# Splitting one tile's load by partitions, with short late copies, in a DMA-bound prefix log-sum-exp kernel

## The chip, the cores and the metric

The kernel runs on one core of one Trainium2 chip. The metric is the device time of one execution in microseconds (us), on the slowest core (here the only one).

## The reference

The input `x` is float32 of shape (4, 4096, 4128). For each of the 4 batches and each of the 4128 columns, the output is the running log-sum-exp down the 4096 rows:

```
out[:, 0, :] = x[:, 0, :]
for t in range(1, S):
    mx = max(out[:, t-1, :], x[:, t, :])
    out[:, t, :] = mx + log(exp(out[:, t-1, :] - mx) + exp(x[:, t, :] - mx))
```

It reads 270.5 MB and writes 270.5 MB, each byte once.

## The kernel before

Each of 44 steps loads one tile: 128 partitions, in each of them `r` consecutive rows of one batch (r is 3 in 40 steps, 2 in 4 steps; the first step has 2). ScalarE (ACT) takes exp, TensorE multiplies by triangular matrices of ones to form the running sums in PSUM (here the tiles `pt` and `qt`, which the matmuls write), and ACT takes the log back into the tile, which is stored. VectorE keeps the last row as a carry for the next step. SP issues all loads and stores on one hardware queue. There are four tile buffers.

```python
    class Step:
        def dram(self, t):
            rows = t[self.b, self.row:self.row + P * self.r, :]
            return rows.rearrange("(p j) d -> p j d", j=self.r)   # partition p: r whole rows

        def load(self):
            full = xpool.tile([P, R, D], FP32, name="xt")
            self.xt = full[:, :self.r, :]
            self.half = self.xt.bitcast(FP16)
            nc.sync.dma_start(out=self.xt, in_=self.dram(x))

        def store(self):
            nc.sync.dma_start(out=self.dram(out), in_=self.xt)
    # ... cut: Chunk, which does exp, the matmuls, the log and the carry ...
    ahead = bufs - 1                       # 3
    for s in steps[:ahead]:
        s.load()
    for n, s in enumerate(steps):
        # ... cut: the compute of the step ...
        s.store()
        if n + ahead < len(steps):
            steps[n + ahead].load()
```

One partition of a three-row tile is one contiguous run of 3 x 4128 x 4 = 49,536 bytes in HBM, and the trace shows it as one DMA packet. A whole tile is 128 packets (10,240 for the 80 three-row transfers), 8 for each of the 16 DMA engines.

The softmax here doesn't subtract the row's maximum and nothing guards it: scores larger than these inputs give would overflow.

## Time and profile before

| | before |
|---|---|
| time, median of 3 (later runs: 1263.1 to 1263.4) | 1263.23 us |
| profiled span | 1261.7 us |
| busy: DMA engines / ACT / TensorE / VectorE | 99% / 77% / 54% / 36% |
| a 49,536-byte packet, median | 1.829 us |
| first exp starts | 13.0 us |
| last store issued | 1243.7 us |

From the page of the kernel before: the mean busy share of the 16 DMA engines in 40 equal slices of the span (tenths), what they moved, and the hardware queue (packets, MB, share of 16 engines' span).

```profile
DMA  9999999999999999999999999999999999999997
GB/s 410 410 443 432 425 432 439 432 428 432 436 433 431 433 436 431 431 438 431 436 434 431 429 432 438 434 429 432 431 440 431 433 430 430 437 433 431 434 429 328
q1 hardware_dynamic: 12672, 541.07, 99.4%
```

The DMA engines are busy in every slice; compute is not what holds the run. The next fence is busy time by stretch: the stretch, its length, then busy us and instruction count of each engine, the granted clock, the busy share of the DMA engines, and GB/s in the last column.

```profile
core 0: us, PE busy (x) PEld busy (x) DVE busy (x) ACT busy (x) POOL busy (x), PEclk, DMA share, GB/s
0.00:34.00 34.00, 11.14 (x27) 3.71 (x28) 11.96 (x15) 19.22 (x15) 2.17 (x13) 1.00 0.95 404
34.00:54.00 20.00, 15.10 (x44) 5.30 (x44) 5.13 (x5) 16.36 (x12) 0.00 (x0) 0.91 1.01 412
54.00:84.00 30.00, 17.83 (x65) 6.48 (x64) 10.54 (x12) 24.46 (x20) 0.00 (x0) 0.77 1.03 446
84.00:1262.00 1178.00, 642.81 (x2135) 230.02 (x2134) 423.81 (x415) 916.58 (x688) 0.00 (x0) 0.75 0.99 430
```

From the page's list of DMA issues of before: KB of one, median us from issue to landing.

```profile
xt<-in_x_dram SPq DMA_DIRECT2D x40, 6192.0 KB, 43.7
xt<-in_x_dram SPq DMA_DIRECT2D x4, 4128.0 KB, 39.1
```

A load lands some 44 us after its issue, three transfers of 14.6 us, so two others are ahead of it in the queue. The chain of waits of before (start, duration, what) shows the first load landing at 13.0 us:

```profile
0.80 12.20 DMA xt<-in_x_dram
```

The queue's issue times on SP (start, duration, line, what), early and late:

```profile
0.80 1.33 SPq L112 DMA_DIRECT2D xt<-in_x_dram  x3
31.72 0.35 SPq L115 DMA_DIRECT2D out_dram<-xt  x1
32.11 0.45 SPq L112 DMA_DIRECT2D xt<-in_x_dram  x1
...
1223.92 20.17 SPq L115 DMA_DIRECT2D out_dram<-xt  x2
```

The last line covers the last two stores, issued at 1223.9 and 1243.7 us.

### The profile page before, as it was taken

The numbers are of one execution on the slowest core, as the hardware profiler recorded it, in microseconds if no ns is written. First come the engines' busy times: TensorE is split into PE (matmuls) and PEld (weight loads), VectorE is DVE, ScalarE is ACT, GpSimd is POOL, SyncE is SP. The second block draws the span as 40 slices with busy tenths as digits, with TensorE's granted clock in tenths as the row PEclk, the third lists the DMA queues.
The fourth block names the chain that finished last, engine by engine and source line by source line (L and its number), as shares of the span: only waits on it lengthen the run. The fifth ranks groups of instructions, "written<-read, shape, count | busy, mean of one in ns | idle before, by whom it ended". The sixth has DMA issues, their size and how long they took to land.

```text
span 1261.7 us, 6165 instructions
## 1 busy us (share of the span) xinstructions
PE 686.9 (54%) x2268; PEld 245.5 (19%) x2268; DVE 451.4 (36%) x445; ACT 976.6 (77%) x733; POOL 2.2 (0%) x13
## 2 busy tenths in 40 slices
PE   3566566566555554545456565554545656545452
PEld 1122222122121221111112222111211212111120
DVE  3433343433333433343333343334333334343333
ACT  5888887888787878778678887877867887787783
POOL 0000000000000000000000000000000000000000
PEclk9977777777677778787667777878766777787876
DMA  9999999999999999999999999999999999999997
GB/s 410 410 443 432 425 432 439 432 428 432 436 433 431 433 436 431 431 438 431 436 434 431 429 432 438 434 429 432 431 440 431 433 430 430 437 433 431 434 429 328
DMA packets 12702, 541.46 MB, mean 429 GB/s; under 512 B 1408, under 2 KB 1408, under 8 KB 1408
## 3 DMA queue, kind: packets, MB, share of 16 engines
q1 hardware_dynamic: 12672, 541.07, 99.4%
q8 instruction: 18, 0.29, 0.1%
q14 instruction: 12, 0.10, 0.0%
HBM read 270.53 MB, written 270.53 MB: 429 GB/s over the span
## 4 chain that ended last, share of the span: by engine, by line
DMA 50%; ACT 25%; PE 20%; issue 2%; DVE 1%; ACTq 0%; SPq 0%
DMA xt<-in_x_dram 29%; DMA out_dram<-xt 21%; PE pt L87 20%; ACT xt L161 13%; ACT xt L127 11%; ACT xt L166 0%; DVE carry L91 0%; DVE carry L92 0%; PE qt L87 0%; ACTq L227 0%; SPq L112 0%; ACTq L127 0%
## 5 line engine op out<-in xcount | busy, mean ns | idle before, releaser
L161 ACT ACTIVATE xt<-pt 128x1024 f32<-128x1024 f32 x512 | 504.7, 1025 | 159.1 <-PE pt L87 87.0
L127 ACT ACTIVATE xt<-xt 128x3072 f16<-128x3072 f32 (+3 forms) x176 | 475.3, 2701 | 76.9 <-DMA xt<-in_x_dram 75.4
L91 DVE CAST carry<-pt 32x1024 f16<-32x1024 f32 x176 | 216.4, 1230 | 695.2 <-ACT xt L161 690.6
L87 PE MATMUL pt<-xt,ident 128*128 128x512 f16 x672 | 235.4, 437 | 313.1 <-ACT xt L161 312.6
L87 PE MATMUL pt<-xt,incl 128*128 128x512 f16 x352 | 157.3, 543 | 242.6 <-ACT xt L127 241.9
L87 PE MATMUL pt<-xt,excl 128*128 128x512 f16 x672 | 263.1, 531 | 0.0
L92 DVE TENSOR_TENSOR carry<-pt,carry 32x1024 f16<-32x1024 f32 x176 | 215.9, 1227 | 6.1
L87 PEld LDWEIGHTS <-ident 128*128 128x128 f16 x672 | 67.0, 103 | 451.1 <-issue 423.0
L87 PEld LDWEIGHTS <-excl 128*128 128x128 f16 x756 | 95.3, 128 | 149.8 <-issue 122.9
L87 PE MATMUL pt<-carry,pick 128*128 128x512 f16 x320 | 119.7, 463 | 0.0
L87 PEld LDWEIGHTS <-incl 128*128 128x128 f16 x480 | 51.8, 112 | 330.6 <-issue 281.2
L87 PEld LDWEIGHTS <-pick 128*128 128x128 f16 x360 | 42.7, 119 | 65.0 <-issue 48.3
L91 DVE CAST carry_t<-qt 32x32 f16<-32x32 f32 x44 | 8.7, 197 | 90.8 <-ACT xt L166 90.7
L166 ACT ACTIVATE xt<-qt 128x96 f32<-128x96 f32 (+1 forms) x44 | 10.9, 249 | 30.3 <-PE pt L87 30.3
L87 PE MATMUL qt<-xt,incl 128*128 128x64 f16 (+2 forms) x128 | 12.2, 195 | 0.0
L87 PE MATMUL qt<-xt,excl 128*128 128x64 f16 (+1 forms) x84 | 10.6, 186 | 0.0
L92 DVE TENSOR_TENSOR carry_t<-qt,carry_t 32x32 f16<-32x32 f32 x44 | 8.5, 194 | 1.5
L87 PE MATMUL qt<-carry_t,pick 128*128 128x96 f16 (+1 forms) x40 | 8.1, 202 | 0.0
L82 DVE MEMSET carry<- 128x512 uint32 x4 | 1.9, 485 | 1.1 <-PEq L216 1.0
L69 ACT ACT_TABLE_LOAD x1 | 1.3, 1283 | 0.8 <-PEq L216 0.8
L35 POOL TENSOR_SCALAR_AFFINE_SELECT pick<-pick 128x128 f16<-128x128 f16 x2 | 0.6, 296 | 0.1
L35 POOL TENSOR_SCALAR_AFFINE_SELECT ident<-ident 128x128 f16<-128x128 f16 x1 | 0.3, 298 | 0.0
(11 smaller groups left out, 1.9 us busy)
## 6 DMA issues: line engine op xcount, KB each, us to landing
xt<-in_x_dram SPq DMA_DIRECT2D x40, 6192.0 KB, 43.7
out_dram<-xt SPq DMA_DIRECT2D x40, 6192.0 KB, 43.5
xt<-in_x_dram SPq DMA_DIRECT2D x4, 4128.0 KB, 39.1
out_dram<-xt SPq DMA_DIRECT2D x4, 4128.0 KB, 34.0
```

The source lines that it names most:

```text
L35: nc.gpsimd.affine_select(out=t, in_=t, pattern=[[step, P]], compare_op=mybir.AluOpType.not_equal, fill=1.0, base=base, channel_multiplier=1,)
L69: nc.scalar.preload_act_table_set("natural_log_exp_and_others")
L82: nc.vector.memset(t, 0.0)
L87: nc.tensor.matmul(pt, lhsT=w, rhs=rhs, start=start, stop=stop, skip_group_check=True)
L91: nc.vector.tensor_copy(cr[HI:HI + 32, :], pt[HI:HI + 32])
L92: nc.vector.tensor_tensor(out=cr[LO:LO + 32, :], in0=pt[HI:HI + 32], in1=cr[HI:HI + 32, :], op=mybir.AluOpType.subtract,)
L127: nc.scalar.activation(self.t.half[:, :, 2 * c0:2 * c0 + w], self.t.xt[:, :, c0:c0 + w], ACT.Exp,)
L161: nc.scalar.activation(t.xt[:, j, c * CH:(c + 1) * CH], pt, ACT.Ln)
L166: nc.scalar.activation(t.xt[:, :, t0:D], self.qt, ACT.Ln)
```

## The change

The intent is to shorten the queue of one DMA engine, which would pay if that engine is the last to finish. The load of the fourth tile is issued at the start, in three pieces: 45 rows (one row is one partition) on POOL's software queue, 80 and 3 rows on SP. The intended shares: 5 packets for one engine, 8 or 9 for the others. Copies of 2 to 15 rows of 64 bytes late in the run are to mark in the trace which engine is which; two such copies on POOL surround the 45 rows.

```diff
+    def small(queue, n):
+        pad = cpool.tile([n, 16], FP32, name=f"pad{n}")
+        queue.dma_start(out=pad, in_=x[0, :n, :16])
-        def load(self):
+        def load(self, uneven=False):
 ...
-            nc.sync.dma_start(out=self.xt, in_=self.dram(x))
+            src = self.dram(x)
+            if not uneven:
+                nc.sync.dma_start(out=self.xt, in_=src)
+                return
+            small(nc.gpsimd, 5)
+            nc.gpsimd.dma_start(out=self.xt[80:125], in_=src[80:125])
+            small(nc.gpsimd, 12)
+            nc.sync.dma_start(out=self.xt[:80], in_=src[:80])
+            nc.sync.dma_start(out=self.xt[125:], in_=src[125:])
 ...
+    steps[ahead].load(uneven=True)
+    probes = list(range(2, 16))
 ...
         s.store()
-        if n + ahead < len(steps):
+        if len(steps) - n <= 8:
+            for _ in range(2):
+                if probes:
+                    small(nc.sync, probes.pop(0))
+        if ahead < n + ahead < len(steps):
             steps[n + ahead].load()
```

## The prediction

> **What bounds the kernel now.** The 16 DMA engines. The DMA row of the 40 slices reads 9 in every slice but the last, queue q1 is busy 99.4% of 16 engines' span (queue table), 429 GB/s mean; ACT, the busiest compute engine, is at 77%. In the trace's DMA packet records an undisturbed 49,536-byte packet takes 1.829 us. An engine carries 704 packets (640 of these, 64 of 33,024 bytes at 1.222 us): about 1249 us, plus completion packets, of the 1261.7 us span.
>
> **What the change aims at.** I followed the packets of each engine as a chain (next start = last end) and compared landings. The engines drift apart. At the next-to-last store the slowest landed 9.2 us after the fastest, the second 7.2, the third 6.0, most others 3 to 5. The slowest loses about 0.1 us per transfer through the whole run (its packets average 1.837 us, slow ones left out, against 1.830); the second lost 5.6 us in the first 650 us in the same way. Instruction fetches (16 KB, 1.05 us each, 18 of them) hit engines in turn and explain most of the rest. The last store is issued at 1243.7 us (SP timeline); fast engines have idled 2.5 to 3.3 us by then and end at about 1254.4, the second slowest at 1258.4, the slowest at 1260.4. So the end is the slowest engine's backlog.
>
> **What is removed, added, moved.**
> - One engine loses 3 packets: 3 x 1.83 = 5.5 us. Three others gain one each, 1.83 us (128 = 80 + 45 + 3 rows: 16x5, 15x3, 3x1). [...]
> - If the relieved engine is the slowest one, its end falls to about 1255, but the second slowest, 1258.4, then ends last: the gain is the difference, about 2.0 us, not 5.5. If that one is among the three with an extra packet, nearly nothing is gained. If another engine is relieved: 0, or 1.8 us worse when the slowest gets an extra packet. I can't number the engines from this trace; I give 0.45 to a hit.
> - The fourth load is issued at the start, not after store 0 at 32.1 us. No bubble was there to fill: store 0 was queued at 31.7 while load 2 was still landing (about 43). The early rows interleave with load 0 and can delay its landing, 13.0 us, by up to 3 x 1.83 = 5.5 us; compute starts that much later, but until about 330 us it is ahead (27.3 us per step against 29.3 of DMA), so DMA keeps work queued and this costs nothing at the end.
> - 15 or so short copies: at most some 0.1 us each on an engine and 0.35 us each on SP (issue time as for large ones). A load is issued with two transfers (29 us) ahead of it in the queue, so SP's delay is hidden.
>
> **Prediction.** 1262.2 us, 80% range 1260.6 to 1264.4. Faster by over 2%: 0.01; within 2%: 0.985; slower: 0.005.
>
> **What would show it.** Final landing spread: the slowest chain down from 9 to about 4 us behind, the second at 7 now last (hit); or the slowest chain unchanged and another one 5.5 us early (miss). First exp starting after 13.0, up to 18.5. DMA row still 9; the last store issued within 2 us of 1243.7.
>
> **What would make it wrong.** Early rows on the other queue starving the SP queue; an underfilled queue around 60 to 100 us; short copies that cost microseconds, not tenths; instruction fetches falling on other engines (1.05 us each).

1263.2 us less 0.45 x 2.0 us is 1262.3, about the forecast of 1262.2. No run had shown the shares 16x5, 15x3 and 3x1 then; later ones do. The 88 transfers of before leave 1,408 packets of 4 bytes (9 ns each), 16 a transfer, which I take to be the completion packets, one from each engine. e3's page shows 1,426 such small packets: 18 more fits 34 (16 + 15 + 3) for the three pieces in place of 16. And in the change POOL's 45 packets start in three rounds of 15 (at 8.9 to 10.3, 16.2 to 18.1 and 24.6 to 26.7 us).

## The result, and the profile after

The changed kernel takes 1285.75 us (median of 4, 1285.66 to 1286.56) against 1263.17 us: ratio 1.0179, 95% interval 1.0162 to 1.0197. Ratios are the mean time of one kernel's runs over that of the other's of the same rounds, so not quite the ratio of the medians. Executions over 1.5% slower than the fastest of the same kernel are left out of the means. The run is 22.6 us slower, where about 1 us faster was predicted.

From the page after: GB/s in 40 slices, and the two queues (hardware, software).

```profile
DMA  9999999999999999999999999999999999999997
GB/s 226 396 322 434 429 435 431 436 433 433 431 435 433 432 435 433 433 431 430 435 431 435 435 433 431 434 433 432 436 432 433 433 434 432 434 432 433 431 433 328
q1 hardware_dynamic: 12868, 538.85, 98.3%
q0 software_dynamic: 128, 2.23, 1.1%
```

The engines are as busy as before, but in the first and third slice they move 226 and 322 GB/s, against 410 and 443. From the fourth slice on the two rows differ by a few GB/s, up and down. The same stretches as before:

```profile
0.00:34.00 34.00, 0.00 (x0) 0.10 (x1) 1.96 (x5) 1.67 (x2) 3.77 (x16) 1.00 0.97 231
34.00:54.00 20.00, 11.14 (x27) 3.58 (x27) 9.41 (x10) 16.96 (x14) 0.00 (x0) 1.00 1.00 433
54.00:84.00 30.00, 18.06 (x57) 6.43 (x57) 11.02 (x11) 24.86 (x19) 0.00 (x0) 0.89 1.00 280
84.00:1285.00 1201.00, 655.96 (x2185) 234.80 (x2183) 428.98 (x420) 933.05 (x701) 0.00 (x0) 0.75 1.00 430
```

The busy share stays at 0.97 to 1.00 while the rate falls to 231 and then 280 GB/s. So the loss isn't idle time. The packets themselves take longer. After 84 us the rate is 430 GB/s in both kernels, which leaves no room there for a loss of 22 us.

The pieces of the fourth load in the list of DMA issues after:

```profile
xt<-in_x_dram SPq DMA_DIRECT2D x1, 3870.0 KB, 80.3
xt<-in_x_dram POOLq DMA_DIRECT2D x1, 2176.9 KB, 30.0
```

The POOL piece, 2.2 MB, was 30 us on its way. The chain of waits after:

```profile
0.81 32.78 DMA xt<-in_x_dram
```

The first load lands at 33.6 us instead of 13.0. The issue times on SP after:

```profile
2.19 0.53 SPq L126 DMA_DIRECT2D xt<-in_x_dram  x1
2.77 0.46 SPq L127 DMA_DIRECT2D xt<-in_x_dram  x1
52.30 28.27 SPq L130 DMA_DIRECT2D out_dram<-xt  x2
...
1267.51 0.37 SPq L130 DMA_DIRECT2D out_dram<-xt  x1
```

SP issues its pieces of the fourth load at once, the first store at 52.3 us (31.7 before), and the last store at 1267.5 us, 23.8 us later than before.

The DMA packet records of the trace say which packets grew. In this table, "excess" is the time of the packets above 1829 ns per 49,536 bytes, summed and divided by 16 engines, for packets that start in the first 110 us:

```
kernel  queue   packets                         took, median (range) ns   excess, us per engine
before  SP      all, 0 to 110 us                1829 for 49,536 bytes      1.95
after   POOL    the 45 rows, 9 to 32 us         5345 (3351 to 6171)        9.55
after   SP      those beside them, 0 to 36 us   mostly 1222 or 1829, some  5.34
                                                2000 to 5600
after   SP      36 to 110 us, the 80 rows       3711 (3126 to 3826)       10.55
                (63 of the 80, clear of others)
```

After minus before is 25.4 - 2.0 = 23.5 us, against 23.2 us of span. The packets of these pieces, and of what shared the engines with them, hold the whole loss. Before, 17 of 10,240 packets of that size took over 2.5 us; after, 141.

### The profile page after: what moved, and what is told of

Its sections match the earlier page's. It is cut to its first block, busy times and chain, and to the rows that moved or that the text cites. A ratio compares the mean times of both kernels' runs of the same rounds, so it can differ in the third digit from the quotient of the medians.

```text
span 1284.9 us, 6184 instructions
## 1 busy us (share of the span) xinstructions
PE 685.2 (53%) x2268; PEld 244.9 (19%) x2268; DVE 451.4 (35%) x445; ACT 976.5 (76%) x733; POOL 3.8 (0%) x16
## 4 chain that ended last, share of the span: by engine, by line
DMA 57%; ACT 21%; PE 18%; issue 2%; DVE 0%; ACTq 0%; SPq 0%
DMA xt<-in_x_dram 33%; DMA out_dram<-xt 24%; PE pt L87 18%; ACT xt L176 11%; ACT xt L142 9%; ACT xt L181 0%; DVE carry L91 0%; DVE carry L92 0%; PE qt L87 0%; ACTq L248 0%; ACTq L142 0%; SPq L119 0%
```

## The experiments

My theory, called P in the expectations: the packets of a DMA that covers only part of the partitions take longer, by an amount that depends on which partitions it covers. Why that should be, no run here measures. The trace of the change shows a halved or worse rate (186 GB/s from 13 to 34 us, 222 from 64 to 80, against some 430), but it can't tell P from the rivals: S, the software queue is slow in itself; C, the short copies hold up the queue; O, the new order of the fourth load and the first store starves it; N, odd or uneven row counts are slow; D, any DMA of fewer than 128 partitions is slow.

All eleven kernels gave correct results.

| run | what differs from the kernel before | time, us | its before, us | ratio, 95% interval |
|---|---|---|---|---|
| e1 | short late copies only | 1263.69 | 1263.13 | 1.0005 (0.9988 to 1.0022) |
| e2 | fourth load early, whole | 1263.10 | 1263.13 | 0.9999 (0.9984 to 1.0014) |
| e3 | early, 45 + 80 + 3 rows, all on SP | 1284.76 | 1263.13 | 1.0170 (1.0155 to 1.0185) |
| e4 | early, a column third on POOL, rest on SP | 1263.36 | 1263.13 | 1.0001 (0.9986 to 1.0016) |
| e5 | early, partitions 0-63 and 64-127 | 1277.69 | 1263.24 | 1.0116 (1.0101 to 1.0131) |
| e6 | early, 0-31, 32-95, 96-127 | 1270.61 | 1263.24 | 1.0059 (1.0044 to 1.0074) |
| e7 | the halves of e5 in four ordinary loads | 1322.30 | 1263.24 | 1.0467 (1.0452 to 1.0483) |
| e8 | the change without the late copies | 1286.36 | 1263.24 | 1.0184 (1.0167 to 1.0201) |
| e9 | six copies of 5 rows added | 1267.02 | 1263.41 | 1.0028 (1.0015 to 1.0042) |
| e10 | six copies of 4 rows added | 1263.31 | 1263.41 | 1.0000 (0.9987 to 1.0012) |
| e11 | as e6, but 32-95 on POOL | 1270.18 | 1263.41 | 1.0054 (1.0040 to 1.0068) |

### e1 and e8: the short copies

```diff
 # e1: the kernel before, plus only the copies after the late stores
+        if len(steps) - n <= 8:
+            for _ in range(2):
+                if probes:
+                    small(nc.sync, probes.pop(0))
 # e8: the changed kernel without these four lines
```

> The short copies alone, on the kernel before. Theory P[...]: within 1.5 us of the kernel before, as the short copies take 11 ns a packet. Rival C (short copies delay the queue): part of the 22.6 us, at least 3 us.

> The whole change without the 14 late short copies (the two early ones on POOL stay). P: as the change, 22 to 24 us slower than before. C: less.

The copies alone change nothing that the rounds resolve (+0.6 us of medians). The change without them is as slow as with them. Rival C falls.

### e2: the early load alone

```diff
-            small(nc.gpsimd, 5)
-            nc.gpsimd.dma_start(out=self.xt[80:125], in_=src[80:125])
-            small(nc.gpsimd, 12)
-            nc.sync.dma_start(out=self.xt[:80], in_=src[:80])
-            nc.sync.dma_start(out=self.xt[125:], in_=src[125:])
+            nc.sync.dma_start(out=self.xt, in_=src)
```

> The fourth load issued at the start, whole, on the SP queue; no split and no short copies. P: within 1.5 us of the kernel before, all packets at 1.83 us. Rival O (the new order of load 3 and store 0 starves the queue around 60 to 100 us): at least 5 us slower.

The time is that of the kernel before. Rival O falls: issuing the fourth load ahead of the first store neither helps nor hurts.

### e3 and e4: is it the software queue?

```diff
 # e3: no POOL
-            nc.gpsimd.dma_start(out=self.xt[80:125], in_=src[80:125])
+            nc.sync.dma_start(out=self.xt[80:125], in_=src[80:125])
 # e4: POOL loads a third by columns, all partitions
+            nc.gpsimd.dma_start(out=self.xt[:, :1], in_=src[:, :1])
+            nc.sync.dma_start(out=self.xt[:, 1:], in_=src[:, 1:])
```

> The same three pieces (45, 80 and 3 rows), all on the SP queue, no short copies, nothing on POOL. P: the 45-row packets still take 3 to 5.6 us and the 80-row packets 3.7, so 15 to 21 us slower than before. Rival S (the software queue is what is slow): only the 80-row piece stays slow, 9 to 11 us slower than before, and the 45-row packets take 1.83 us.

> POOL loads one third of the fourth tile by columns (all 128 partitions, 16,512 bytes of each, 2.11 MB against 2.23 MB), SP the other two thirds, both early; no short copies. P: packets at the full rate (16,512 bytes in 0.61 us), within 2 us of the kernel before. S: packets of the software queue two to three times as long, about 13 us slower.

Busy time by stretch, e3 first, e4 second:

```profile
0.00:34.00 34.00, 9.29 (x30) 3.40 (x31) 12.18 (x15) 20.59 (x16) 2.16 (x13) 0.97 0.95 404
34.00:54.00 20.00, 15.00 (x49) 5.39 (x48) 4.91 (x4) 15.88 (x12) 0.00 (x0) 0.72 1.21 272
54.00:84.00 30.00, 17.02 (x56) 6.08 (x55) 11.39 (x13) 24.78 (x20) 0.00 (x0) 0.77 0.87 224
```

```profile
0.00:34.00 34.00, 8.16 (x27) 3.01 (x28) 10.36 (x14) 17.70 (x15) 2.76 (x14) 1.00 0.98 415
34.00:54.00 20.00, 13.71 (x39) 4.81 (x39) 5.93 (x6) 17.75 (x12) 0.00 (x0) 0.67 0.97 419
54.00:84.00 30.00, 18.54 (x68) 6.80 (x67) 11.02 (x11) 23.82 (x18) 0.00 (x0) 0.76 1.02 428
```

In e3 the 45 rows come after load 2 on the same queue, so the first 34 us are as before (404 GB/s). The loss moves to 34 to 84 us, and the whole run loses 21.6 us without any software queue. Its 45-row packets took about 6 us each, somewhat more than I had expected (3 to 5.6), its 80-row packets 3.7. In e4 POOL moved nearly as many bytes as in the change (2,064 KB, 128 packets of 16,512 bytes) at 0.615 us a packet, the full rate, and the run is as fast as before. In e4 the first load landed at 16.1 us, 3 us late, and that cost nothing. Rival S falls; e11 tests it once more with rows of the change's length.

### e5, e6 and e7: which partitions

```diff
 # e5 (early) and e7 (in the loop, for the 4th, 14th, 24th and 34th load)
+            nc.sync.dma_start(out=self.xt[:64], in_=src[:64])
+            nc.sync.dma_start(out=self.xt[64:], in_=src[64:])
 # e6
+            nc.sync.dma_start(out=self.xt[:32], in_=src[:32])
+            nc.sync.dma_start(out=self.xt[32:96], in_=src[32:96])
+            nc.sync.dma_start(out=self.xt[96:], in_=src[96:])
```

> Fourth load early on the SP queue as two DMAs: partitions 0 to 63, then 64 to 127. P[...] every packet takes 3.66 us, 8 x 1.83 = 14.6 us slower than before. Rival N (odd row counts or uneven shares per engine are slow, not the partitions): 64 rows are 4 for each of 16 engines, so within 2 us of before.

> As e5, but three DMAs: partitions 0 to 31, 32 to 95, 96 to 127. P: the middle one has 64 rows too[...] its packets take 1.83 us; the outer two (32 rows, 2 per engine[...]) take 3.66 us; together 4 x 1.83 = 7.3 us slower than before, half of e5. Rival D (any DMA with fewer than 128 partitions is slow): as much as e5 or more. N: within 2 us of before.

> As e5, but at the ordinary place in the loop, for four loads (the 4th, 14th, 24th and 34th). P: four times the cost of e5, 4 x 14.6 = 58 us slower, so the cost does not depend on the early phase. Rival (the cost belongs to the start of the run, where compute has not begun): clearly less than 58.

The 3.66 us of the expectations is twice the 1.83 us of an undisturbed packet. The factor two, and that 32 to 95 would run at the full rate, were my estimates.

The packet records of the fourth load, median time of a packet in each round of 16 (one for each engine), leaving out the first and those in which one piece passes into the next:

```
e5   0 to 63: 3.87 us     64 to 127: 3.87 us
e6   0 to 31: 3.88 us     32 to 95: 1.83 us     96 to 127: 3.87 us
```

GB/s in 40 slices of e5 and of e6, from their pages. A slice is 32 us, and the dips are in the second and third one:

```profile
GB/s 406 273 380 432 431 426 438 432 433 430 437 432 432 435 432 434 430 437 431 429 433 438 430 437 426 438 429 440 430 430 433 436 431 436 426 443 426 442 429 333
```

```profile
GB/s 408 325 432 425 430 434 432 433 435 429 433 434 428 437 433 430 438 430 432 433 430 436 431 435 436 427 438 433 432 434 432 434 430 436 433 431 434 433 432 332
```

A DMA of 64 rows is slow on partitions 0 to 63 and at full speed on 32 to 95. Row count, packet size, packets per engine, queue and source layout are the same; only the partitions differ, and with them the rows of `x` that are read. Rival D falls, and rival N for pieces of 64 rows. The costs fit: 14.5 us for two halves (14.6 expected), 7.4 us for e6 (7.3 expected), 59.1 us for four loads in halves (58 expected, 14.8 each). That e5 fits so closely is in part luck: at 3.87 us, 8 packets would lose 16.3 us, but the first round of each half was faster (3.2 to 3.75 us), and the excess of e5's packets over those of before is 14.9 us. The cost does not depend on the phase of the run: the engines have no idle time to hide it (DMA row 9 in every slice but the last).

Rows 32 to 63 of the tile go to the same partitions in e5 and in e6: they took 3.87 us a packet together with 0 to 31, and 1.83 us together with 64 to 95. So neither a row's place in HBM nor its partition is slow in itself; what counts is which ones are loaded together.

What sets the sizes for the change's own pieces was not shown. In e3 none of the 128 packets of the fourth load took under 2.87 us: all engines slowed alike. The 45 rows took about 6 us there, the 80 rows 3.7, the 64 rows of each half of e5 3.87. No run isolates this, and none loads 45 or 80 rows onto other partitions.

### e11: the software queue on partitions 32 to 95

```diff
 # as e6, but
+            nc.gpsimd.dma_start(out=self.xt[32:96], in_=src[32:96])
```

> As e6, but partitions 32 to 95 are loaded by POOL (software queue), 0 to 31 and 96 to 127 by SP, all early. P: the POOL rows take 1.83 us each although they interleave with load 0, the outer pieces 3.9; together 7 to 8 us slower than before, like e6. Rival S: the 64 POOL rows take 4 to 6 us each, at least 15 us slower.

POOL's 64 packets took 1829 ns (1829 to 1833), interleaved with the first loads; the outer pieces, on SP, were the slow ones (351 GB/s from 54 to 84 us, against 446 before). Busy time by stretch:

```profile
0.00:34.00 34.00, 7.98 (x18) 2.61 (x19) 6.00 (x9) 13.73 (x10) 2.73 (x14) 1.00 0.95 404
34.00:54.00 20.00, 13.42 (x38) 4.71 (x37) 6.17 (x7) 16.07 (x11) 0.00 (x0) 1.00 1.10 396
54.00:84.00 30.00, 17.77 (x57) 6.14 (x56) 10.21 (x10) 24.63 (x19) 0.00 (x0) 0.72 0.95 351
```

The first load landed at 20.7 us, 7.7 us later than before, yet the whole run lost only 6.8 us (medians), no more than e6 lost (7.4 us) without any such delay. So a late start of compute is free here, as predicted.

### e9 and e10: which engine ends the run, and does it matter

The short copies do their work as markers. In the trace of the change the 14 copies left 119 packets of 64 bytes, n for the copy of n rows. The copies pass in pairs (2 and 3 rows, 4 and 5, up to 14 and 15). In each pair the engines show two packets 12 to 13 ns apart, one engine only one: 2 and 1 engines in the first pair, 4 and 1 in the second, 14 and 1 in the last. Followed as chains (next start = last end), an engine that one copy reached is reached by every later one: the one with a single packet at 1113.9 us has two at 1143.2, 1172.4 and so on. So I number the engines in the order in which the copies reach them: an engine that gets the copy of 5 rows but not that of 4 is engine 4 (0 and 1 can't be told apart). In e1, which is the kernel before plus markers, the packet records show the next-to-last store landing like this:

```
e1, next-to-last store, us after the fastest engine; then the end of the engine's last transfer
engine 4     8.4    1260.3
engine 13    6.3    1258.3
engine 14    5.4    1257.3
engine 15    2.0    among 1255.9 to 1256.0
all others   4.0 or less
```

```diff
+    scratch = [nc.dram_tensor(f"scratch{i}", (5, D), FP32).ap() for i in range(6)]   # e10: 4 rows
 ...
         s.store()
+        if 18 <= n < 24:
+            nc.sync.dma_start(out=scratch[n - 18][:, :4096], in_=x[0, :5, :4096])
```

> Kernel before plus six copies of 5 rows of 16,384 bytes, DRAM to DRAM, one after each of six stores in mid-run. If a copy of 5 rows runs on engines 0 to 4, and engine 4 is the one that ends last (as the short copies of e1 show), engine 4 carries 6 x 0.61 = 3.6 us more and the run ends 3.6 us later. Rival (the end is not one engine's backlog; only total bytes count): 0.98 MB written at 433 GB/s, 2.3 us at most, and the same per byte in e10.

> As e9 with 4 rows, so engines 0 to 3 carry 3.6 us more each and engine 4 nothing. If engine 4's backlog ends the run: within 0.7 us of the kernel before, as engines 0 to 3 were at least 4 us ahead of engine 4 at the end of e1. Rival: four fifths of e9.

By their pages e9 has 60 packets more on the queue than before (12,732 against 12,672) and e10 48 (12,720): 5 or 4 of data for each copy, and as many of under 512 bytes. By the markers, 5 rows are engines 0 to 4. Six packets more for these (0.611 us each) made the run 3.6 us longer; the same for engines 0 to 3 changed nothing. So the backlog of engine 4 does end the run of the kernel before, and the prediction was right to count in packets of the slowest engine. I didn't expect so clean a result. The expectation's 0.98 MB counts reads and writes: the 30 rows are 0.49 MB written, so the rival allowed even less than 2.3 us.

Then which engine did the change relieve? In its trace, at the third-last store, one engine landed at 1243.9 us, 6.1 us ahead of the next one (1249.9) and 15.2 us ahead of the last (1259.0). It is the one engine that got no short copy at all, not even that of 15 rows: engine 15. It was relieved and saved the run nothing, because it was not behind: in e1 engine 15 was 2.0 us behind the fastest. Engine 4 still ended late (1282.1 us), and the last one (1283.5 us) was engine 0 or 1, which had the copy of 2 rows and, by the markers, an extra packet of the 3-row piece. POOL's 45 packets, in three rounds of 15, leave out one engine; that it was 15 is inferred from its lead.

No run relieved engine 4. The pieces that reach a chosen set of engines are the ones with few rows: by the markers, copies from SP go to the lowest numbers (5 rows: 0 to 4), so they can load engine 4 but not spare it alone, and of the pieces of whole rows that I loaded only 32 to 95 did not slow down. A POOL piece that skips engine 4 was not tried. The gain on offer is also small: with engine 4 out of the way, engine 13 would have ended e1 at 1258.3 instead of 1260.3, at most 2.1 us or 0.16% (estimated from the ends above). So I ran no version meant to beat both kernels, and none of those that ran does so clear of noise.

## Why the prediction was wrong

- **"What bounds the kernel now": right.** The DMA engines bound it; every us of packet time added to all engines (e5, e7), or to the last one (e9), came out as about a us of run time (14.9 us of packets and 14.5 of run in e5, 3.7 and 3.6 in e9).
- **"The end is the slowest engine's backlog": right**, shown by e9 and e10.
- **The step that failed: the term "3 x 1.83 = 5.5 us" for the early rows, and with it the silent assumption that the 80 rows cost what 80 rows of a whole tile cost.** I costed every packet at the 1.829 us that the trace of before showed. There, all loads cover 128 partitions. The 45-row packets took 5.3 us and the 80-row packets 3.7 us. It is not the queue (e3: about 6 and 3.7 us on SP alone); that the partitions covered decide is shown for pieces of 64 rows (3.87 us in e5, 1.83 in e6), and for 45 and 80 rows it is my inference. Packets beside the 45 rows were held up too (5.3 us per engine). That is 23.5 us of engine time against 0 in the prediction, and the measured loss is 22.6 us. The trace of before has no load of fewer partitions that could have shown this.
- **"First exp starting after 13.0, up to 18.5": wrong for the same reason**, 33.6 us. **"This costs nothing at the end": right for the delay as such.** In e11 compute began 7.7 us late and e11 cost no more than e6. What costs is the longer packets, not the later start.
- **"If the relieved engine is the slowest one" (0.45): it was not.** Engine 15 was relieved, engine 4 is the slow one, and engine 0 or 1, which got an extra packet, ended last. Even the hit would have been worth 2 us against a cost of 23.
- **"Short copies: at most some 0.1 us each": right in effect**; 11 ns a packet, and e1 shows no change. The early issue in place of the late one was worth nothing, as predicted (e2).
- **"DMA row still 9": right, and misleading.** The row shows busy time. It stayed at 9 while the rate halved (226 GB/s in the first slice, 410 before). The list of what would make the prediction wrong named a starving or underfilled queue, which I took to show as idle engines; it did not name longer packets.

What stays open: the runs show which partitions are slow together (0 to 63, 64 to 127, 0 to 31, 96 to 127) and by how much (3.87 or 3.88 us against 1.83 for 32 to 95), but not why. Why all engines slow alike (e3) is open. Why the slow packets take 3.87 us and not 3.66 (twice 1.83) is not settled, nor is why engines 4 and 13 are behind in the kernel before.

## What to carry to other kernels

Cost a DMA by the partitions that it covers, not by bytes and rows alone: in a kernel whose DMA engines are never idle, cutting one tile's load into two partition halves cost 14.5 us, while cutting it by columns, or as partitions 32 to 95, ran at full rate (0.615 us for 16,512 bytes, 1.83 for 49,536). When the busy row stays full and the run gets longer, compare GB/s and the time of single packets. Before relieving an engine, find out by marker copies and a deliberate overload of a few packets which one ends last, how far the next is behind it, and which engine your split in fact relieves.
